# Four tiles of a convolution's output normed beside its second chunk, two of them kept in DRAM in between

## The chip, the cores and the metric

The kernel runs on one core of a Trainium2 chip. The time is that of one launch on the device, in microseconds (us), as the median of several runs. Profiles are single executions recorded by the hardware; their times count from the first instruction.

## The reference

One step of a two-layer backbone. There are 256 context tokens (the prompt, "p") and 2048 latent tokens ("s"), 1024 channels, all in float32. Layer 0 is a gated convolution branch, layer 1 is neighbourhood attention; both end in an output projection that is scaled by a gate and added to the residual. The change lies in layer 0:

```python
def conv_branch(h, w_in, dw_w, dw_b, ln_g, ln_b, w_out):
    a, b, z = jnp.split(h @ w_in, 3, axis=-1)
    u = a * jax.nn.sigmoid(b)
    u = lax.conv_general_dilated(u, dw_w[:, None, :], ...,     # 31 taps along the tokens,
        feature_group_count=CONV_WIDTH) + dw_b                 # each channel by itself
    u = layer_norm(u, ln_g, ln_b)
    u = jax.nn.silu(u) * jax.nn.silu(z)
    return u @ w_out

x = x + gate * conv_branch(rms_norm(x) * (1 + scale) + shift, ...)
```

## The kernel before

Matrix products run at full precision as three products of float32r halves (high x high, high x low, low x high), so every operand exists as a "hi" and a "lo" tile. TensorE multiplies; the others prepare operands and take results out of PSUM.

**The convolution (`conv_layer`).** The tokens are worked in two chunks: the prompt with latent tokens 0 to 1023, then latent tokens 1024 to 2047. In each chunk the 1024 channels are taken in eight steps of 128. A step projects a, b and z (the `ci_ps` products, L360 to L362) into two PSUM banks in turn, ScalarE applies the sigmoid (L474), VectorE multiplies (L476), z goes to DRAM (`zc_d`). The 31 taps are then summed: pairs as differences on VectorE into two PSUM accumulators (`cv`, L530 and L532, pool `acc`), the rest as scaled copies on ScalarE (L509) and additions on GpSimd (L512). Two joins (L536) put them together, and the result goes to DRAM (`vc_d`, L539). The steps are written as events with times on a clock of their own; sorting them gives the order of the instructions on TensorE, ScalarE, VectorE and GpSimd, which is kept (`manual_schedule`). SyncE issues the loads and stores, in an order that the scheduler chooses.

**The norm (`norm_stages`).** For a tile of 128 tokens it loads the convolution's output v and z from DRAM (L706, L708; these need the stores of all eight steps), sums over channels (L712), spreads the mean by a matmul with a matrix of ones (L720), subtracts it (L722), squares (L725), sums again (L712), gets the variance (L731), the reciprocal root (L734 to L737) and spreads it (L740), scales (L744), applies SiLU to z (L742) and to v (L747), multiplies both (L753), and rounds the product y into its hi and lo halves on GpSimd (`round_pool` L105, `rest_pool` L108). It is a generator with stages, so that a caller can lay the stages between other work.

Two prompt tiles are normed within the second chunk: `LN_FIRST`, `LN_GAP` and `LN_TIMES` place their stages on the events' clock. They use three of the four parts of a work buffer (`ln_work`), their y goes to `ln_y`. The first latent tile is normed behind `conv_layer` by `conv_norm` (L760), in the same work buffer, and its y takes two of the `t4` tiles, of which there are eight (`"t4": 8`, 4 KB per partition each). The conv weights, the gates (one for the prompt, one for the latent tokens) and wide norms use `t4` too.

**The output pipeline (`conv_out_pipeline`).** Eight tiles of 128 tokens (the prompt's two, then latent tokens 0 to 767) are projected by `w_out`, one in each pass of the loop (variable `i`). A pass holds 48 matmuls in four quarters (L848 and L849 with yh, L851 with yl), the residual additions of two halves (L857, L858), the store of x1, the root mean square of the result, and transposes (L304) for the next layer. Between the quarters stand the stages of the norms of later tiles: the loop starts tile i + 3, and tile i + 3's mean is the first of TensorE's matmuls in pass i + 1. The order on TensorE is the written one; the other engines are ordered by the scheduler. These norms take v and y from `t4`, z from `raw`, and PSUM from the pool `lnps`, which is opened when `acc` is closed. Residual tiles (`x1`) of passes 0 and 1 lie in `t4`, those of later passes in `xp`, a pool that is opened after the taps' buffers (`convp`) are closed.

Of the kernel before, what the change touches and what calls it, by code (L numbers as in the profile page):

```python
# [11 lines left out]
F32 = mybir.dt.float32  # L12
F32R = mybir.dt.float32r
# [5 lines left out]
P = 128  # L19
D = 1024  # L20
NK = D // P
# [17 lines left out]
DVE_PACE = 1.1  # L39
ADA_TIME = 3.1  # L40
ACT_FIRST = 0.5
LN_FIRST = 2
LN_GAP = 66.0
LN_TIMES = (0, 6, 14, 18, 21, 25, 33, 37, 47, 49, 52, 54, 54.1, 60, 62)
ADA_AHEAD = 4.0
ADA_LAG = 3.5
LEAD = 1.9
# [28 lines left out]
class Kern:  # L76
    def __init__(self, ctx, tc, io):
        self.tc, self.nc, self.io = tc, tc.nc, io
        self.ctx = ctx
        self.more, self.more_bufs, self.turn = None, 0, 0  # L80
        self.cp = ctx.enter_context(tc.tile_pool(name="consts", bufs=1))
        self.dr = ctx.enter_context(tc.tile_pool(name="scratch", bufs=1, space=bass.MemoryType.DRAM))
        d = lambda name, shape: self.dr.tile(shape, F32, name=name, tag=name)
        self.zc_d = d("zc_d", [D, NTOK])
        self.wl_d = d("wl_d", [3 * NK, P, D])
        self.vc_d = d("vc_d", [2, D, VCOLS // 2])
        self.x1_d = d("x1_d", [NTOK, D])
        self.qh_d = d("qh_d", [D, NTOK])
        self.ql_d = d("ql_d", [D, NTOK])
        self.ks_d = d("ks_d", [NH, 2, DH, NTOK])  # L90
        self.vp_d = d("vp_d", [NPR, NH, 2, DH])
        self.vs_d = d("vs_d", [GW // CW, NSA // GW, CW, NH, 2, DH])
        self.bm_d = d("bm_d", [NH, 3, P, 3, 480])
        self.zn_d = d("zn_d", [D, NTOK])
        self.kc_d = d("kc_d", [NH, 2, DH, NCTX])
        self.cvs_d = d("cvs_d", [NCTX, NH, 2, DH])
        self.w2_d = d("w2_d", [2, D, D])
        self.x2_d = d("x2_d", [NTOK, D])
        self.gate_d = d("gate_d", [2, 2, D])
        self.rpb_d = d("rpb_d", [P + 1, RPB_PITCH])  # L100
        self.yp_d = d("yp_d", [NK, 2, P, NPR])


    def round_pool(self, out, src):
# [260 lines left out]
    def conv_layer(self, part_a, part_b):  # L365
# [7 lines left out]
        at = lambda t, f: events.append((t, len(events), f))  # L373
# [257 lines left out]
        at(begin[NK] + 1, room)  # L631

        self.ready = []
        for j in range(2):

            st = {}

            def norm(st=st, j=j):
                if "g" not in st:
                    work, y = self.room  # L640
                    st["g"] = self.norm_stages("p", P * j, self.ready, [work[:, i] for i in range(3)] + [y[:, 2 * j + i] for i in range(2)])
                next(st["g"], None)

            for dt in LN_TIMES:
                at(begin[NK + LN_FIRST] + 2 + LN_GAP * j + dt, norm)
# [42 lines left out]
        for _, _, f in sorted(events, key=lambda e: e[:2]):  # L688
            f()

    def norm_stages(self, src, t0, y, room=None, wide=False):


        nc = self.nc
# [60 lines left out]
        yh, yl = room[3:] if room else (self.t4(F32R, nm + t) for t in ("_yh", "_yl"))  # L755
        self.round_pool(yh, z)
        self.rest_pool(yl, z, yh)
        y.append((yh, yl))

    def conv_norm(self, src, t0, room=None):  # L760
        y = []
# [63 lines left out]
    def conv_out_pipeline(self, w, blocks, ready, ahead, res):  # L825
# [39 lines left out]
        for i in range(len(tiles) + 2):  # L865
            src, a = names[i]
            run = i < len(tiles)
            if run:
                x1[i] = self.t4(F32, f"x1_{src}{a}", [P, D]) if i < 2 else self.xp.tile([P, D], F32, tag="ln", name=f"x1_{src}{a}", bufs=5)
                nc.sync.dma_start(x1[i], self.tok_rows(src, a, P))  # L870
            t, before = i + 2, i + 1
            norm(t + 1, True)
            if run:
                pm = self.mm_bank(f"co_{src}{a}_0")
            if i == 0:
                quarter(i, 0, 0, pm)
                norm(t, True)
                norm(t)
            norm(t)
            norm(before)  # L880
            if 0 < i < len(tiles):
                quarter(i, 0, 0, pm)
            norm(t)
            norm(before)
            norm(t)
            norm(before)
            scale = None
            if last:
                residual(*last)
            norm(t)  # L890
            more()
            if run:
                quarter(i, 0, 1, pm)
            norm(t)
            norm(before)
            norm(t)
            if last:
                scale = self.store_x1(i - 1, names[i - 1], x1, tiles, prep, res)
                last = None
            norm(before)  # L900
            if run:
                residual(i, 0, pm)
                more()
                pm = self.mm_bank(f"co_{src}{a}_1")
                quarter(i, 1, 0, pm)
            norm(t)
            more()
            if run:
                quarter(i, 1, 1, pm)
                last = i, 1, pm  # L910
            norm(t)
            if scale:
                scale()
            norm(t + 1)
            more()
# [427 lines left out]
    def phase1(self):  # L1343
        tc = self.tc
        with ExitStack() as c:
# [5 lines left out]
            with tc.tile_pool(name="convp", bufs=2) as self.up, tc.tile_pool(name="acc", bufs=2, space=bass.MemoryType.PSUM) as self.pc:  # L1351
# [2 lines left out]
                with tc.manual_schedule(engines=ordered):  # L1354
                    self.conv_layer([("p", 0, 256), ("s", 0, 512), ("s", 512, 512)], [("s", 1024, 512), ("s", 1536, 512)])
                work = self.room[0]
                self.ready.append(self.conv_norm("s", 0, [work[:, i] for i in range(3)] + [self.t4(F32R, f"ln_s0_y{t}") for t in "hl"]))
                self.gate = [self.spread_row(self.t4(F32, f"gate0_{g}", [P, D]), self.gate_d[0, g]) for g in range(2)]
                w = [[], []]
                for _ in self.out_weight(self.io["conv_w_out"][0], "co", w):  # L1360
# [474 lines left out]
```

## Time and profile before

| | |
|---|---|
| median of 3 runs | 2816.69 us (2813.48 to 2820.18) |
| profiled execution | 2823.78 us, span 2821.9 us, granted TensorE clock 0.984 |
| TensorE busy | 2699.2 us, 96% of the span |
| VectorE, ScalarE, GpSimd busy | 1764.9, 1377.1, 1392.8 us |
| DMA | 533.86 MB, mean 189 GB/s |

Times in the profile are microseconds from the span's start. PE is TensorE, PEld its weight loads, DVE VectorE, ACT ScalarE, POOL GpSimd, SP SyncE, and SPq its queue, which issues DMAs. L706 is line 706 of the kernel before. A row of the timeline has start, duration, engine, line, operation, output and inputs, and in brackets the idle time before it and what ended it. Tiles are named without their numbers, so that `ln_s` is any norm of latent tokens.

### The profile page before, as it was taken

The numbers are of one execution on the slowest core, as the hardware profiler recorded it, in microseconds if no ns is written. First come the engines' busy times: TensorE is split into PE (matmuls) and PEld (weight loads), VectorE is DVE, ScalarE is ACT, GpSimd is POOL, SyncE is SP. The second block draws the span as 40 slices with busy tenths as digits, with TensorE's granted clock in tenths as the row PEclk, the third lists the DMA queues.
The fourth block names the chain that finished last, engine by engine and source line by source line (L and its number), as shares of the span: only waits on it lengthen the run. The fifth ranks groups of instructions, "written<-read, shape, count | busy, mean of one in ns | idle before, by whom it ended". The sixth has DMA issues, their size and how long they took to land.

```text
span 2821.9 us, 45216 instructions
## 1 busy us (share of the span) xinstructions
PE 2699.2 (96%) x16079; PEld 2336.9 (83%) x16079; DVE 1764.9 (63%) x3046; ACT 1377.1 (49%) x2436; POOL 1392.8 (49%) x1569
## 2 busy tenths in 40 slices
PE   6999999999899999999999999989999999899998
PEld 4888877776777889999998888878888898788887
DVE  4678778888885610012456522368787787778885
ACT  3446454456453322234222244256676676667764
POOL 4687776566454343355123235134455454455564
PEclk9999999999999999999999999999999999999999
DMA  7233554555546554446789986688676768966763
GB/s 256 68 128 113 180 189 151 166 185 186 166 115 179 159 159 135 127 146 194 240 297 337 364 245 192 206 227 221 180 199 197 195 176 207 243 186 181 199 167 109
DMA packets 445337, 533.86 MB, mean 189 GB/s; under 512 B 79665, under 2 KB 322441, under 8 KB 444984
## 3 DMA queue, kind: packets, MB, share of 16 engines
q1 hardware_dynamic: 440368, 510.11, 61.3%
q10 hardware_dynamic: 4744, 20.85, 1.9%
q8 instruction: 128, 2.10, 0.3%
q14 instruction: 97, 0.79, 0.1%
HBM read 355.14 MB, written 179.79 MB: 190 GB/s over the span
## 4 chain that ended last, share of the span: by engine, by line
PE 73%; DMA 10%; DVE 5%; SPq 4%; ACT 3%; POOL 3%; issue 3%; POOLq 0%; ACTq 0%; DVEq 0%
PE sa_T L1603 7%; PE ci_ps L360 6%; PE ci_ps L361 6%; PE ci_ps L362 6%; PE sa_O L1632 5%; PE sa_O L1627 4%; PE ni_s L361 4%; PE ni_s L362 4%; PE ni_s L360 4%; PE sa_S L1571 4%; PE sa_S L1570 3%; PE o L1725 2%; PE o L1727 2%; PE o L1726 2%; DMA bm_d<-bm 2%
## 5 line engine op out<-in xcount | busy, mean ns | idle before, releaser
L1597 POOL TENSOR_SCALAR sa_p<-sa_p,sa_m 128x992 f32<-128x992 f32 (+2 forms) x256 | 276.8, 1081 | 431.5 <-DVE sa_m L1596 304.7
L512 POOL TENSOR_TENSOR cv_p<-cv_p,cv_p 128x640 f32<-128x640 f32 (+1 forms) x240 | 359.1, 1496 | 120.6 <-ACT cv_p L509 107.7
L1612 ACT CAST sa_pt<-sa_T 128x512 fp32r<-128x512 f32 (+3 forms) x512 | 275.3, 588 | 211.3 <-PE sa_T L1603 208.3
L111 DVE TENSOR_TENSOR sa_pt<-sa_T,sa_pt 128x512 fp32r<-128x512 f32 (+3 forms) x512 | 328.5, 683 | 2.4 <-ACT sa_pt L1612 2.2
L360 PE MATMUL ci_ps<-h_s_hi,ci_wh 128*128 128x512 f32 x768 | 308.9, 402 | 7.5 <-ACT z L479 3.7
L361 PE MATMUL ci_ps<-h_s_lo,ci_wh 128*128 128x512 f32 x768 | 304.2, 396 | 0.0
L362 PE MATMUL ci_ps<-h_s_hi,ci_wl 128*128 128x512 f32 x768 | 304.2, 396 | 0.0
L1595 ACT ACTIVATE sa_p<-sa_S,sa_m 128x992 f32<-128x992 f32 (+2 forms) x256 | 267.1, 1043 | 57.0 <-DVE sa_m L1591 49.4
L1603 PE MATMUL sa_T<-ident,sa_p 128*128 128x128 f32 (+3 forms) x2048 | 273.6, 276 | 9.7 <-DVE sa_pt L111 9.3
L1589 DVE TENSOR_REDUCE sa_m<-sa_S 128x1 f32<-128x512 f32 x256 | 176.2, 688 | 165.5 <-PE sa_S L1571 153.4
L1603 PEld LDWEIGHTS sa_T<-ident,sa_p 128*128 128x128 f32 (+3 forms) x2048 | 238.3, 138 | 47.1 <-issue 16.8
L509 ACT ACTIVATE cv_p<-u,ws 128x640 f32<-128x640 f32 (+1 forms) x256 | 190.8, 777 | 134.2 <-DVE u L476 98.6
L532 DVE SCALAR_TENSOR_TENSOR cv<-u,dw,cv 128x640 f32<-128x640 f32 (+1 forms) x240 | 196.2, 817 | 0.5
L1632 PE MATMUL sa_O<-sa_pt,a_v 120*128 120x256 f32 (+5 forms) x1280 | 190.7, 279 | 0.0
L360 PEld LDWEIGHTS ci_ps<-h_s_hi,ci_wh 128*128 128x128 f32 x768 | 146.2, 190 | 47.6 <-ACT z L479 6.9
L532 DVE SCALAR_TENSOR_TENSOR cv<-cv_d,dw,cv 128x640 f32<-128x640 f32 (+1 forms) x224 | 182.8, 816 | 0.0
L1627 PE MATMUL sa_O<-sa_pt,cv 128*128 128x256 f32 x1024 | 175.8, 294 | 5.3 <-ACT sa_pt L1612 1.1
L1591 DVE CUSTOM_DVE_ANT_0 sa_S<-sa_S,a_bm,sa_m 128x480 f32<-128x480 f32 (+2 forms) x256 | 170.9, 668 | 9.0
L362 PEld LDWEIGHTS ci_ps<-h_s_hi,ci_wl 128*128 128x128 f32 x768 | 145.9, 190 | 34.0
L361 PEld LDWEIGHTS ci_ps<-h_s_lo,ci_wh 128*128 128x128 f32 x768 | 146.4, 191 | 31.2
L1632 PEld LDWEIGHTS sa_O<-sa_pt,a_v 120*128 120x128 f32 (+2 forms) x1280 | 167.3, 191 | 0.0
L360 PE MATMUL ni_s<-h_s_hi,nis_wh 128*128 128x512 f32 x384 | 150.5, 392 | 2.2 <-ACT ni_s_f L1032 1.4
(798 smaller groups left out, 7143.0 us busy)
## 6 DMA issues: line engine op xcount, KB each, us to landing
adaw<-in_ada_w SPq DMA_DIRECT2D x24, 1024.0 KB
ci_w<-in_conv_w_in SPq DMA_DIRECT2D x48, 512.0 KB
a_bm<-bm_d SPq DMA_DIRECT2D x32, 720.0 KB
x_s<-in_x_sample SPq DMA_DIRECT2D x32, 512.0 KB
vs_d<-v_s SPq DMA_DIRECT2D x128, 128.0 KB
a_qh<-qh_d SPq DMA_DIRECT2D x128, 128.0 KB
a_ql<-ql_d SPq DMA_DIRECT2D x128, 128.0 KB
o_x<-x_d SPq DMA_DIRECT2D x32, 512.0 KB
```

The lines of the kernel that those rows point to most:

```text
L111: self.nc.vector.tensor_tensor(out=lo, in0=src, in1=hi.bitcast(F32), op=ALU.subtract)
L360: self.nc.tensor.matmul(out, wh[:, k, :], hh[:, k, :], start=k == 0, stop=False)
L361: self.nc.tensor.matmul(out, wh[:, k, :], hl[:, k, :], start=False, stop=False)
L362: self.nc.tensor.matmul(out, wl[:, k, :], hh[:, k, :], start=False, stop=k == NK - 1)
L512: nc.gpsimd.tensor_tensor(out=st["t", 0], in0=st["t", 0], in1=st["t", j], op=ALU.add)
L532: nc.vector.scalar_tensor_tensor(out=st["acc", b], in0=d, scalar=w, in1=st["acc", b], op0=ALU.mult, op1=ALU.add)
L1595: nc.scalar.activation(p[:, n], S[:, n], AF.Exp, scale=-1.0, bias=m[:, 2:3], accum_out=m[:, 3:4])
L1597: nc.gpsimd.tensor_scalar(out=p[:, n], in0=p[:, n], scalar1=m[:, 3:4], scalar2=1.0, op0=ALU.mult, op1=ALU.mult)
L1603: nc.tensor.transpose(t[:w, c * P : c * P + P], p[:, x + c * w : x + c * w + w], self.ident)
L1612: nc.scalar.copy(pt[:w, 0, part, :, at], t)
L1627: nc.tensor.matmul(o, cv[:, c].rearrange("p s d -> p (s d)"), x, start=s + c == 0, stop=False)
L1632: nc.tensor.matmul(dst, v[:w, c0 + c].rearrange("p s d -> p (s d)"), loc[:, lo:hi], start=False, stop=s == 1 and c == 3)
```

## The change

- The norms within the second chunk are four instead of two: the prompt's tiles and latent tokens 0 to 127 and 128 to 255. They begin one step earlier (`LN_FIRST` 1), follow each other at 48 instead of 66, and their stages are closer by the same ratio.
- The y of the two new tiles is written into the third and fourth part of the work buffer (the third also holds the squares) and stored in DRAM (`y_d`, four stores of 512 KB, `put_away`). In the pipeline, one pass ahead of its use, each is fetched into two `xp` tiles (four loads of 512 KB in all).
- The norm behind the convolution is that of latent tokens 256 to 383, the pipeline's fifth tile. The norms within the pipeline begin with its sixth tile, so that passes 0 and 1 hold no norm, and there are five instead of seven.
- Residual tiles of passes 0 to 3 lie in `t4`, not only those of 0 and 1.

```diff
@@ -39,9 +39,9 @@
 DVE_PACE = 1.1
 ADA_TIME = 3.1
 ACT_FIRST = 0.5
-LN_FIRST = 2
-LN_GAP = 66.0
-LN_TIMES = (0, 6, 14, 18, 21, 25, 33, 37, 47, 49, 52, 54, 54.1, 60, 62)
+LN_FIRST = 1
+LN_GAP = 48.0
+LN_TIMES = (0, 4.5, 10.5, 13.5, 16, 19, 25, 28, 35.5, 37, 39.5, 41, 41.1, 45.5, 47)
 ADA_AHEAD = 4.0
 ADA_LAG = 3.5
 LEAD = 1.9
@@ -99,6 +99,7 @@
         self.gate_d = d("gate_d", [2, 2, D])
         self.rpb_d = d("rpb_d", [P + 1, RPB_PITCH])
         self.yp_d = d("yp_d", [NK, 2, P, NPR])
+        self.y_d = d("y_d", [2, 2, P, D])
 
 
     def round_pool(self, out, src):
@@ -631,14 +632,15 @@
         at(begin[NK] + 1, room)
 
         self.ready = []
-        for j in range(2):
+        for j, (src, t0) in enumerate((("p", 0), ("p", P), ("s", 0), ("s", P))):
 
             st = {}
 
-            def norm(st=st, j=j):
+            def norm(st=st, j=j, src=src, t0=t0):
                 if "g" not in st:
                     work, y = self.room
-                    st["g"] = self.norm_stages("p", P * j, self.ready, [work[:, i] for i in range(3)] + [y[:, 2 * j + i] for i in range(2)])
+                    to = [y[:, 2 * j + i] for i in range(2)] if j < 2 else [work[:, i].bitcast(F32R) for i in (3, 2)]
+                    st["g"] = self.norm_stages(src, t0, self.ready, [work[:, i] for i in range(3)] + to, then=None if j < 2 else self.put_away)
                 next(st["g"], None)
 
             for dt in LN_TIMES:
@@ -688,7 +690,21 @@
         for _, _, f in sorted(events, key=lambda e: e[:2]):
             f()
 
-    def norm_stages(self, src, t0, y, room=None, wide=False):
+    def put_away(self, yh, yl):
+
+        at = self.y_d[len(self.ready) - 2]
+        for s, y in enumerate((yh, yl)):
+            self.nc.sync.dma_start(at[s], y.bitcast(F32).rearrange("p k t -> p (k t)"))
+
+        def fetch():
+            ys = [self.xp.tile([P, NK, P], F32R, tag="ln", name=f"ln_back{s}", bufs=5) for s in "hl"]
+            for s, y in enumerate(ys):
+                self.nc.sync.dma_start(y.bitcast(F32).rearrange("p k t -> p (k t)"), at[s])
+            return tuple(ys)
+
+        return fetch
+
+    def norm_stages(self, src, t0, y, room=None, wide=False, then=None):
 
 
         nc = self.nc
@@ -755,7 +771,7 @@
         yh, yl = room[3:] if room else (self.t4(F32R, nm + t) for t in ("_yh", "_yl"))
         self.round_pool(yh, z)
         self.rest_pool(yl, z, yh)
-        y.append((yh, yl))
+        y.append(then(yh, yl) if then else (yh, yl))
 
     def conv_norm(self, src, t0, room=None):
         y = []
@@ -866,10 +882,12 @@
             src, a = names[i]
             run = i < len(tiles)
             if run:
-                x1[i] = self.t4(F32, f"x1_{src}{a}", [P, D]) if i < 2 else self.xp.tile([P, D], F32, tag="ln", name=f"x1_{src}{a}", bufs=5)
+                x1[i] = self.t4(F32, f"x1_{src}{a}", [P, D]) if i < 4 else self.xp.tile([P, D], F32, tag="ln", name=f"x1_{src}{a}", bufs=5)
                 nc.sync.dma_start(x1[i], self.tok_rows(src, a, P))
             t, before = i + 2, i + 1
             norm(t + 1, True)
+            if out.get(before) and callable(out[before][0]):
+                out[before] = [out[before][0]()]
             if run:
                 pm = self.mm_bank(f"co_{src}{a}_0")
             if i == 0:
@@ -1354,7 +1372,7 @@
                 with tc.manual_schedule(engines=ordered):
                     self.conv_layer([("p", 0, 256), ("s", 0, 512), ("s", 512, 512)], [("s", 1024, 512), ("s", 1536, 512)])
                 work = self.room[0]
-                self.ready.append(self.conv_norm("s", 0, [work[:, i] for i in range(3)] + [self.t4(F32R, f"ln_s0_y{t}") for t in "hl"]))
+                self.ready.append(self.conv_norm("s", 2 * P, [work[:, i] for i in range(3)] + [self.t4(F32R, f"ln_s256_y{t}") for t in "hl"]))
                 self.gate = [self.spread_row(self.t4(F32, f"gate0_{g}", [P, D]), self.gate_d[0, g]) for g in range(2)]
                 w = [[], []]
                 for _ in self.out_weight(self.io["conv_w_out"][0], "co", w):
```

## The prediction

> **What bounds the kernel now.** I read the page first (busy shares, then the chain that ended last), then the busy time by stage around the places where the diff works, then what TensorE waited for there, and last the rows of the engines behind the longest wait.
>
> ```profile
> PE 2699.2 (96%) x16079; PEld 2336.9 (83%) x16079; DVE 1764.9 (63%) x3046; ACT 1377.1 (49%) x2436; POOL 1392.8 (49%) x1569
> ```
> ```profile
> PE 73%; DMA 10%; DVE 5%; SPq 4%; ACT 3%; POOL 3%; issue 3%; POOLq 0%; ACTq 0%; DVEq 0%
> ```
>
> TensorE is busy for 96% of the span and carries 73% of the chain. A change elsewhere is worth only what it takes from TensorE's remaining idle time, or puts there. The diff works in three stretches: the second chunk of the convolution (about 440 to 717 us), the tail of the taps (717 to 737), and the pipeline of eight output tiles (717 to 837). I call one pass of the pipeline's loop a round, and number the tiles of 128 tokens 0 to 9 in the loop's order: 0 and 1 are the prompt, 2 is latent token 0, and so on.
>
> ```profile
> core 0: us, PE busy (x) PEld busy (x) DVE busy (x) ACT busy (x) POOL busy (x), PEclk, DMA share, GB/s
> 696.00:737.00 41.00, 29.81 (x121) 23.59 (x121) 39.87 (x48) 18.29 (x24) 23.73 (x13) 0.90 0.61 190
> 717.00:737.00 20.00, 11.38 (x51) 9.00 (x49) 19.40 (x25) 4.32 (x5) 3.52 (x3) 0.87 0.55 160
> 739.00:749.00 10.00, 10.00 (x41) 8.14 (x40) 4.67 (x7) 2.10 (x3) 2.86 (x4) 0.84 0.70 264
> 763.00:789.00 26.00, 25.49 (x125) 20.64 (x124) 23.44 (x29) 16.13 (x33) 16.73 (x20) 1.00 0.54 135
> 789.00:837.00 48.00, 43.62 (x206) 35.50 (x204) 38.25 (x45) 25.26 (x51) 25.06 (x30) 0.96 0.41 114
> ```
>
> The columns are the stretch, its length and each engine's busy time, then granted clock, DMA share and GB/s. From 696 to 737 VectorE is full (39.87 of 41) while TensorE is not; from 717 TensorE has only 11.38 of 20. Later both are nearly full. What TensorE waited for between 717 and 900 (total, times, longest):
>
> ```profile
> PE ln_s_mu L720 <- DVE cv_p L536: 8.6, 1, 8.6
> PE ln_s_rb L740 <- DVE ln_s_dg L737: 3.1, 2, 2.6
> PE ln_s_var L731 <- DVE ln_s_s L712: 2.1, 4, 1.3
> ```
>
> One wait is larger than the rest together. TensorE's own rows show where it sits:
>
> ```profile
> 717.21 0.40 PE L848 MATMUL co_p<-co_h,ln_y 128*128 128x512 f32 x1
> ...
> 727.30 1.07 PE L851 MATMUL co_p<-co_h,ln_y 128*128 128x512 f32 x4
> 737.00 0.80 PE L720 MATMUL ln_s_mu<-ln_s_s,ones 128*128 128x128 f32 x2 [8.62 <-DVE cv_p L536]
> ```
> ```profile
> 751.18 0.38 PE L720 MATMUL ln_s_mu<-ln_s_s,ones 128*128 128x128 f32 x2
> ```
> ```profile
> 763.04 0.27 PE L720 MATMUL ln_s_mu<-ln_s_s,ones 128*128 128x128 f32 x1
> ```
> ```profile
> 776.07 0.27 PE L720 MATMUL ln_s_mu<-ln_s_s,ones 128*128 128x128 f32 x1
> ```
> ```profile
> 788.92 0.27 PE L720 MATMUL ln_s_mu<-ln_s_s,ones 128*128 128x128 f32 x1
> ```
> ```profile
> 800.78 0.55 PE L740 MATMUL ln_s_rb<-ln_s_dg,ones 128*128 128x128 f32 x1 [2.61 <-DVE ln_s_dg L737]
> ```
> ```profile
> 805.64 0.27 PE L720 MATMUL ln_s_mu<-ln_s_s,ones 128*128 128x128 f32 x1
> ```
>
> Round 0 lasts from 717.21 to 728.37 (11.2 us). Round 1 opens with the mean of tile 3 (L720), and waits 8.62 us for the last join of the taps (L536): the norms' PSUM banks are opened where the taps' accumulators lay. From then on rounds begin at L720: 751.18, 763.04, 776.07, 788.92, 805.64. Round 1 took 14.18 us and round 2, with as many matmuls and no wait, 11.86: the wait leaves 2.3 us of slower matmuls behind it. So 10.9 us is the most that the removal of this wait gives.
>
> **The change, part by part.**
>
> *Two more norms in the second chunk.* Tiles 2 and 3 (latent tokens 0 to 255) are normed there, tile 4 takes the place of tile 2 after the taps. What one norm costs is in the rows of the work buffer (count, then min/median/max in ns; L712 is a sum, L722 and L744 take off the mean and scale, L753 multiplies by the gate path):
>
> ```profile
> L712 DVE TENSOR_REDUCE ln_p_s<-ln_work x4: 1979/2016/2036, 496.7 to 587.0; 128x128 f32<-128x1024 f32 x4
> ...
> L753 DVE TENSOR_TENSOR ln_work<-ln_work x3: 1226/1668/1886, 553.9 to 677.1; 128x1024 f32<-128x1024 f32 x3
> L722 DVE TENSOR_TENSOR ln_work<-ln_work,ln_p_mu x2: 1211/1211/1211, 509.6 to 578.4; 128x1024 f32<-128x1024 f32 x2
> L744 DVE TENSOR_TENSOR ln_work<-ln_work,ln_p_rb x2: 1211/1211/1211, 546.4 to 615.1; 128x1024 f32<-128x1024 f32 x2
> ```
>
> VectorE: two sums at 2.0, two passes at 1.2, one at 1.7, about 8.1 us; ScalarE the squares and SiLU; GpSimd two passes for y; SyncE three loads and now two stores of 512 KB. Two norms add some 16 us of VectorE over about 200 us, and the cover there is VectorE's wait for TensorE:
>
> ```profile
> DVE u L476 <- PE ci_ps L362: 29.3, 11, 5.1
> ```
> ```profile
> PE ci_ps L360 <- ACT u L474: 1.8, 1, 1.8
> PE ci_ps L360 <- DVE shift L248: 1.1, 1, 1.1
> ```
>
> 29.3 us in 11 waits, so the arithmetic is hidden. Not hidden are the collisions of queues in written order: with two norms in this stretch TensorE lost 1.8 us behind ScalarE's sigmoid and 1.1 us behind VectorE, 2.9 us; two more could cost as much again or nothing. I take +1.5 (0 to 5, the upper end with the matmul slowdown that followed the 8.62 us wait added). If the cover is gone, VectorE's L476 is late, the two matmul banks stay full and TensorE waits for them. The stores and the fetches, 8 x 512 KB, pass on a DMA that is 0.5 to 0.7 busy; on SyncE's queue each stands behind GpSimd's rest pass, where weight loads queue behind it; the code asks for those 13 to 18 us ahead of use, so I cost that at nothing (0 to 1).
>
> *No norm in rounds 0 and 1.* The first norm in the pipeline is now tile 5, loaded in round 2, with its mean at the head of round 3. The 8.62 and 2.3 us go: -10.9, and round 1 can end at 728.4 + 11.2 = 739.6.
>
> *Tiles 2 and 3 come back from DRAM.* Round 2 needs both halves of tile 2, which are fetched into buffers that lie where the taps' were. The nearest rows are the loads into that space now:
>
> ```profile
> 736.97 0.32 SPq L539 DMA_DIRECT2D vc_d<-cv_p  x1
> 739.09 2.28 SPq L870 DMA_DIRECT2D x_s<-in_x_sample  x5
> 752.10 1.00 SPq L706 DMA_DIRECT2D ln_s_v<-vc_d  x2
> ```
> ```profile
> 763.01 0.36 SPq L706 DMA_DIRECT2D ln_s_v<-vc_d  x1
> ```
> ```profile
> 850.31 5.80 DMA x_s<-in_x_sample
> ```
>
> The last store of the taps is issued at 736.97 and the first load into their space at 739.09, 2.1 us later. Five loads of 512 KB then pass at 264 GB/s, 2.0 us each; another load of x_s is 5.8 us on the chain. So a fetch lands 2.0 to 5.8 us after 739.09; I take 4.0, between. Then the taps end later: tile 4's norm needs tile 3's work buffers, which the written schedule frees 29 us later than it frees tile 1's for tile 2 now (349.8 + 144 + 47 against 384.2 + 66 + 62 on its own clock), and brings its whole 8.1 us of VectorE into the full stretch that ends at 737, where tile 2 leaves about 3 (the L744 and L753 passes and a small one). That is +5 if all of it comes before the last tap and 0 if none: I take 2.6. Round 2 then begins at 739.1 + 2.6 + 4.0 = 745.7, a wait of 6.1, and with 2.3 us of slow matmuls behind it +8.4 (ends: +1.4 without slowdown, with the early landing and taps as now, and +13 with 5.8 and 5). Behind the waiting matmul stand all of round 2's, in TensorE's fixed order, and the residual adds on VectorE wait for them; behind the waiting fetch on SyncE's queue stand the loads of later tiles, which have a round to spare.
>
> *Four residual tiles and the fifth's y in the eight t4 buffers.* This is the place I trust least. Rows on who gets a buffer:
>
> ```profile
> 751.38 0.69 DVE L857 TENSOR_TENSOR co_op<-co_p,gate 128x512 f32<-128x512 f32 x1 [1.05 <-PE co_p L851]
> ```
> ```profile
> 778.48 1.23 DVE L753 TENSOR_TENSOR ln_s_z<-ln_s_v,ln_s_z 128x1024 f32<-128x1024 f32 x1
> ```
> ```profile
> 762.16 2.40 POOL L108 TENSOR_TENSOR ln_s_yl<-ln_s_z,ln_s_yh 128x1024 fp32r<-128x1024 f32 x1 [1.62 <-PE co_s L849]
> ```
> ```profile
> 772.64 0.38 PE L740 MATMUL ln_s_rb<-ln_s_dg,ones 128*128 128x128 f32 x2
> ```
>
> The load of tile 5 at 752.10 followed the last use of the prompt's gate (751.38), tile 3's yl (762.16) and tile 6's load (763.01) followed TensorE's last reads of tile 2: t4 is full, and buffers go out in program order. In the new round 3 it must hold one gate, y of tile 4 (2), the residual tiles 0 to 3 (4) and the inputs of tiles 5 and 6 (2): nine. The ninth gets its buffer only when tile 5's input is done. Tile 5's L740 in round 3 (763.04) is at 772.64 and its last product L753 at 778.48 to 779.7: 16.7 us after the round began, where the round itself lasts 13.0. If the ninth is tile 4's yl, it is late by 3.7 + 2.4 (L108) less the 1.8 us of matmuls that open the round, 4.3, and some of that is gained because VectorE is less loaded: I take 3.2, slow matmuls included (0 to 6). If it is tile 6's input, see the rivals.
>
> A page of the Trainium skill bears on the slow matmuls ("TensorE: Matmul & The Clock Gate", Part 1): the clock is halved only after an idle window of about 3.4 us. By it waits of 2 to 3 us would cost their length alone and this term 2.2 instead of 3.2. The trace speaks against a firm bound: the round with the 2.61 us wait (800.78) lasted 16.72 against 12.85 for the one before, 1.3 us more than the wait.
>
> *Later rounds.* Rounds 5 to 7 fill the stretch from 789 to 837, 48 us where three rounds of 13 are 39: TensorE's small waits (L740 3.1, L731 2.1) and slow matmuls behind them make most of the 9. With two norms less in the queue of GpSimd and VectorE part of it may go; the same buffers may bring a new wait in round 5, when tile 7's input needs the buffer of residual 0. I take -2 (-9 to +3).
>
> **Sum.** -10.9 + 8.4 + 3.2 + 1.5 - 2.0 = +0.2 us against the profiled execution's own 2823.78 (span 2821.9). That execution stands 7.1 us above the median shown, 2816.69; what changes is a local difference, so I carry it over: about 2817. After the pipeline nothing is touched, and a shift of TensorE passes to the end, since it is near full throughout. A difference of 0.2% (5.6 us) is about what a measurement of this kernel can tell from no change; the three runs shown spread by 6.7.
>
> **Rivals.**
>
> *Faster: the buffers do not bite.* If the residual of tile 3 gives way, or GpSimd and VectorE finish tile 5 within the round, the 3.2 is gone; if also the taps end at 737 as now, the fetch costs 3.5 and 2.3 of slow matmuls, and the later rounds give 4: -10.9 + 5.8 + 1.5 - 4 = -7.6, 2809; with every bound the good way -14, 2803. For it: from 763 to 789 VectorE has 23.44 of 26 with a norm in every round, so with none it has room in rounds 0 to 2. Against: tile 5's chain hangs on matmuls at fixed places of TensorE's order, which less load does not move.
>
> *Slower: tile 6's input is the ninth.* The residual tile 3 stands before it in the program, so it would take the gate's buffer, and tile 6 would wait for tile 5's product, 3.7 us past the end of round 3. Then two loads (2 to 4 us) and a sum (2.0 us) stand before the mean at the head of round 4, which TensorE cannot pass: 3.7 + 3 + 2 = 8.7, less some 1.4 for a lighter VectorE, with 2.3 behind it +9.6 in place of 3.2. The sum is +6.6, 2823; with late taps and collisions in the chunk +13, 2830. It decides as soon as this wait passes 9 us. For it: the order of the rows above. Against: tile 4's y may be ready so late that it is the ninth.
>
> *The change does nothing there.* If the fetch waits for another part of the old space, or late taps hold round 2 until about 751, the wait has only moved from round 1 to round 2: -10.9 + 13 + 1.5 = +3.6, 2820, still no change.
>
> **How the numbers follow.** No change 0.38 (the forecast, with the moved wait in it), faster 0.31, slower 0.31: the two rivals hang on the same buffers, and the rows do not say which user comes ninth. Those two ends give 2803 and 2830; I leave out a tenth at each side: 2804 to 2829. The forecast alone would range from 2812 to 2822.
>
> **What would show it.** Right: no L720 wait in round 1; round 1 begins at once after round 0; L848 at the head of round 2 waits 3 to 9 us for the fetched tile, whose loads are issued some 2 us after the last store of the taps; the last L536 comes 0 to 5 us later against the end of the convolution's matmuls; a wait at the head of round 4, for yl (then L851) or for the mean (then L720). In the chunk VectorE's waits at L476 shrink from 29.3 by about 16, TensorE's grow by less than 5. The prediction is wrong if round 2 begins with no wait, or if in round 4 there is none, or if VectorE in the chunk comes to hold TensorE's banks.

## The result, and the profile after

The changed kernel takes 2849.01 us (median; 2847.83 to 2855.09) beside 2815.09 for the kernel before in the same comparison: a ratio of 1.0136, 95% interval 1.0113 to 1.0158. It is slower by 34 us between these medians (the recorded ratio, which is not their quotient of 1.0120, would make it 38); the forecast was 2817, with a range of 2804 to 2829. The profiled execution of the changed kernel spans 2846.0 us. All line numbers below are those of the changed kernel, which lie higher than those of before: the norm's sum L712 is now L728, its mean matmul L720 is L736, the output products L848 to L851 are L864 to L867, the weights' rest co_l is L112.

The busy shares and the chain of the changed kernel:

```profile
PE 2692.8 (95%) x16079; PEld 2329.0 (82%) x16079; DVE 1763.4 (62%) x3046; ACT 1380.8 (49%) x2438; POOL 1392.5 (49%) x1569
...
PE 35%; DMA 2%; DVE 2%; ACT 1%; issue 1%; SPq 1%; POOL 0%; POOLq 0%; DVEq 0%; ACTq 0%
```

TensorE does the same 16079 matmuls, but the chain, which TensorE carried to 73% before, is followed here through only some two fifths of the span (the shares of its line add up to 42%). So the page alone does not locate the loss; the stages do. First the rows of TensorE that open the second chunk, the pipeline, and the first products after it, in the kernel before and in the changed one:

```profile
447.13 1.06 PE L225 MATMUL ada_ps<-adaw,cs 128*32 128x512 f32 x8
```
```profile
860.36 0.50 PE L360 MATMUL ni_s<-h_s_hi,nip_wh 128*128 128x512 f32 x1
```
```profile
438.44 1.49 PE L226 MATMUL ada_ps<-adaw,cs 128*32 128x512 f32 x12
```
```profile
715.60 0.40 PE L864 MATMUL co_p<-co_h,ln_y 128*128 128x512 f32 x1
```
```profile
882.57 0.39 PE L361 MATMUL ni_s<-h_s_hi,nip_wh 128*128 128x512 f32 x1
```

With 717.21 as the first output product of before, the second chunk lasts 270.1 us before and 277.2 after (+7.1), the pipeline 143.1 and 167.0 (+23.8), and what follows to the end of the span 1961.5 and 1963.4 (+1.9). The stretch ahead of the chunk is 8.7 us shorter in the changed kernel's execution; none of the changed lines works there (the last section returns to it). Without that stretch the stages give +32.8, and the medians +33.9.

What TensorE waited for from 712 to 900 us in the changed kernel (total, times, longest), and two of the stretches shown of before:

```profile
PE ln_s_mu L736 <- DVE ln_s_s L728: 14.7, 2, 10.5
PE co_p L865 <- DVE co_l L112: 11.0, 6, 6.1
PE co_p L864 <- ACT co_h L790: 5.4, 2, 3.7
```
```profile
717.00:737.00 20.00, 6.28 (x12) 3.17 (x12) 19.11 (x23) 5.91 (x7) 8.06 (x5) 0.68 0.62 196
...
763.00:789.00 26.00, 21.45 (x102) 17.47 (x101) 12.54 (x19) 8.31 (x18) 7.83 (x12) 1.00 0.47 150
```

The 8.62 us behind the last join of the taps are gone, and two others stand in their place: 16.4 us (11.0 + 5.4) for the output weights, and 14.7 us for the sum of a norm. From 717 to 737 TensorE does 12 matmuls where it did 51, at a granted clock of 0.68 (0.87 before); from 763 to 789 VectorE is busy for 12.5 of 26 us where it was for 23.4, and no engine is full. The rows of the first rounds:

```profile
716.54 0.39 PE L864 MATMUL co_p<-co_h,ln_y 128*128 128x512 f32 x1
717.96 0.49 PE L865 MATMUL co_p<-co_l,ln_y 128*128 128x512 f32 x1 [1.03 <-DVE co_l L112]
722.16 0.80 PE L864 MATMUL co_p<-co_h,ln_y 128*128 128x512 f32 x1 [3.71 <-ACT co_h L790]
724.28 0.79 PE L865 MATMUL co_p<-co_l,ln_y 128*128 128x512 f32 x1 [1.32 <-DVE co_l L112]
...
728.74 0.50 PE L865 MATMUL co_p<-co_l,ln_y 128*128 128x512 f32 x1 [1.54 <-DVE co_l L112]
...
735.67 0.80 PE L865 MATMUL co_p<-co_l,ln_y 128*128 128x512 f32 x1 [6.08 <-DVE co_l L112]
...
741.21 0.79 PE L865 MATMUL co_p<-co_l,ln_y 128*128 128x512 f32 x1 [0.47 <-DVE co_l L112]
...
744.73 0.39 PE L865 MATMUL co_p<-co_l,ln_y 128*128 128x512 f32 x1
...
749.55 0.39 PE L864 MATMUL co_p<-co_h,ln_y 128*128 128x512 f32 x1
```

Round 0 takes 715.60 to 749.55, 33.95 us, where it took 11.16. In it stand the 16.4 us of waits; the other 6.4 are slow matmuls (0.80 us at 735.67 against 0.39 at 716.54). Round 1 then runs from 749.55 to 760.54 without a wait: 11.0 us in place of 22.8. Then the second new wait, in the order in which it arises (SyncE's queue, VectorE, TensorE):

```profile
784.26 1.00 SPq L722 DMA_DIRECT2D ln_s_v<-vc_d  x2
```
```profile
793.03 1.87 DVE L728 TENSOR_REDUCE ln_s_s<-ln_s_v 128x128 f32<-128x1024 f32 x1 [5.32 <-DMA ln_s_v<-vc_d]
```
```profile
794.96 0.80 PE L736 MATMUL ln_s_mu<-ln_s_s,ones 128*128 128x128 f32 x2 [10.51 <-DVE ln_s_s L728]
```
```profile
813.76 0.76 PE L736 MATMUL ln_s_mu<-ln_s_s,ones 128*128 128x128 f32 x2 [4.18 <-DVE ln_s_s L728]
```

The load of tile 6's values is issued at 784.26, VectorE sums them at 793.03, 8.8 us later, and the mean that opens round 4 waits 10.51 us; the one that opens round 5 waits 4.18. Rounds 3 and 4 together take 42.0 us (771.75 to 813.76) where they took 25.9 (763.04 to 788.92). So the pipeline's +23.8 is +22.8 (round 0), -11.8 (round 1), -0.7 (round 2), +16.1 (rounds 3 and 4) and -2.6 (after them).

Why are the weights late? First the row of the first co_l in the kernel before; then, in the changed kernel, the load that opens the norm behind the taps, that norm's product on VectorE and its last pass on GpSimd, and the first and the last co_l:

```profile
689.86 2.31 DVE L111 TENSOR_TENSOR co_l<-co_raw,co_h 128x1024 fp32r<-128x1024 f32 x1 [0.36 <-POOL ln_s_yl L108]
```
```profile
661.66 0.37 SPq L722 DMA_DIRECT2D ln_work<-vc_d  x1
```
```profile
706.12 1.21 DVE L769 TENSOR_TENSOR ln_work<-ln_work 128x1024 f32<-128x1024 f32 x1
```
```profile
714.40 2.42 POOL L109 TENSOR_TENSOR ln_s_yl<-ln_work,ln_s_yh 128x1024 fp32r<-128x1024 f32 x1
```
```profile
707.25 1.21 DVE L112 TENSOR_TENSOR co_l<-co_raw,co_h 128x1024 fp32r<-128x1024 f32 x1
```
```profile
739.93 1.23 DVE L112 TENSOR_TENSOR co_l<-co_raw,co_h 128x1024 fp32r<-128x1024 f32 x1 [1.04 <-ACT co_h L790]
```

Before, co_l starts at 689.86, 0.36 us of waiting behind the last pass (yl) of tile 2's norm. Now the norm behind the taps (tile 4) begins with its load at 661.66, because it stands behind tile 3's in the same work buffer, and ends at 716.8; co_l starts at 707.25, 17.4 us later, and the eighth at 739.93 (717.37 before): 24.3 us after the first output product, where it started 0.2 us after it. The norm's values lie in the work buffer, which is one of the four "slot" buffers; the output weights need all four. Yet the first co_l does not wait for that buffer here: it follows the norm's product (L769) on VectorE without a pause, and two pieces of it are written by 709.6, while GpSimd reads that product out of the work buffer until 716.8. What sets its time in this trace is its place in VectorE's order, which the scheduler chose, and the trace does not tell why. The fifth experiment gives the norm other buffers.

### The profile page after: what moved, and what is told of

Its sections match the earlier page's. It is cut to its first block, busy times and chain, and to the rows that moved or that the text cites. A ratio compares the mean times of both kernels' runs of the same rounds, so it can differ in the third digit from the quotient of the medians.

```text
span 2846.0 us, 45222 instructions
## 1 busy us (share of the span) xinstructions
PE 2692.8 (95%) x16079; PEld 2329.0 (82%) x16079; DVE 1763.4 (62%) x3046; ACT 1380.8 (49%) x2438; POOL 1392.5 (49%) x1569
## 5 line engine op out<-in xcount | busy, mean ns | idle before, releaser
L1615 POOL TENSOR_SCALAR sa_p<-sa_p,sa_m 128x992 f32<-128x992 f32 (+2 forms) x256 | 277.7, 1085 | 431.1 <-DVE sa_m L1614 300.2
L112 DVE TENSOR_TENSOR sa_pt<-sa_T,sa_pt 128x512 fp32r<-128x512 f32 (+3 forms) x512 | 328.5, 683 | 2.5 <-ACT sa_pt L1630 2.2
L361 PEld LDWEIGHTS ci_ps<-h_s_hi,ci_wh 128*128 128x128 f32 x768 | 145.4, 189 | 52.9 <-ACT u L475 10.4
L363 PEld LDWEIGHTS ci_ps<-h_s_hi,ci_wl 128*128 128x128 f32 x768 | 145.4, 189 | 33.7
```

What stands on the lines that cost most here:

```text
L112: self.nc.vector.tensor_tensor(out=lo, in0=src, in1=hi.bitcast(F32), op=ALU.subtract)
L361: self.nc.tensor.matmul(out, wh[:, k, :], hh[:, k, :], start=k == 0, stop=False)
L363: self.nc.tensor.matmul(out, wl[:, k, :], hh[:, k, :], start=False, stop=k == NK - 1)
L1615: nc.gpsimd.tensor_scalar(out=p[:, n], in0=p[:, n], scalar1=m[:, 3:4], scalar2=1.0, op0=ALU.mult, op1=ALU.mult)
```

## The experiments

**The residual tiles as before.** The change, but only the two prompt tiles' residuals in t4.

```diff
-x1[i] = self.t4(...) if i < 4 else self.xp.tile(...)
+x1[i] = self.t4(...) if i < 2 else self.xp.tile(...)
```

> The changed kernel, but residual tiles 2 and 3 lie in xp again, so that t4 must hold at most eight. Buffers theory (the ninth t4 tile delays tile 6's input, 10.5 us of wait at the head of round 4 and 4.2 in round 5): both waits go, with the slow matmuls behind them some 16 us, so the time is 2831 to 2835, still 16 to 20 above the kernel before, and the waits for the output weights in round 0 (16.4 us) stay. Weights theory alone (all of the loss is the late low halves of the output weights in round 0, and the later waits are only its echo): within 5 us of the changed kernel, 2844 to 2854. A third way: the fifth xp buffer is short now, and residual 3 waits for tile 2's halves, which shows as a new wait in round 3 or 4 and takes back a part.

Measured: 2838.48 us, ratio 1.0101 (1.0077 to 1.0124), 0.35% less than the change, some 10 us. TensorE's waits from 712 to 900:

```profile
PE co_p L865 <- DVE co_l L112: 10.5, 6, 5.6
PE co_p L864 <- ACT co_h L790: 7.3, 3, 3.7
```

The time is 3.5 us above the range of the buffers theory, and the waits are as it said. The wait for the mean is gone, in round 4 and in round 5, and nothing of its size has taken its place; the pipeline is 153.6 us long, 13.4 less. The wait for the weights stays, 17.8 us in sum. So the t4 buffers cost 10 to 13 us, by the mechanism of the slower rival, and they are not the whole.

**No norm behind the taps.** The change without tile 4's norm there (four tiles are normed before the pipeline, tile 4 is its first).

```diff
-self.ready.append(self.conv_norm("s", 2 * P, [work[:, i] for i in range(3)] + ...))
```

> The changed kernel without the norm behind the taps: tile 4 is normed in the pipeline, beginning in round 1. Weights theory (the norm behind the taps holds the work buffer from 626 to 717 us instead of to 690, so that the low halves of the output weights find no place and VectorE makes them 17 us late; 16.4 us of waits in round 0): round 0 takes 11 to 13 us again, round 2 waits 3 to 5 us for the fetched tile, and the wait at the head of round 4 stays; some 15 us less than the changed kernel, 2832 to 2838. Buffers theory alone: round 0 may be whole, but the wait at the head of round 4 grows by as much, 2846 to 2852.

Measured: 2829.24 us, ratio 1.0065 (1.0046 to 1.0083), 0.71% less than the change, some 20 us, and 3 us below the lower end of the weights theory's range. Round 0 now runs through; rounds 2, 4 and 5 wait:

```profile
748.19 0.74 PE L864 MATMUL co_s<-co_h,ln_backh 128*128 128x512 f32 x1 [2.74 <-issue]
```
```profile
780.84 2.08 PE L867 MATMUL co_s<-co_h,ln_s_yl 128*128 128x512 f32 x4 [3.92 <-POOL ln_s_yl L109]
```
```profile
797.85 0.77 PE L736 MATMUL ln_s_mu<-ln_s_s,ones 128*128 128x128 f32 x2 [4.19 <-DVE ln_s_s L728]
```

The fetch of tile 2 (ln_backh, the operand of the waiting matmul; the trace puts the wait down to "issue") holds TensorE for 2.74 us. It is issued at 744.59, 2.1 us behind the last store of the taps at 742.51. This is the wait that the prediction had put into the change, and that the late round 0 hides there. The t4 buffers cost two waits here. Round 4 waits 3.92 us for the low half of tile 4's y: its high half is made at 765.43, and GpSimd begins the low one at 778.45, just behind tile 5's product on VectorE (777.00 to 778.22). Round 5 waits 4.19 us for a mean. The third experiment, with fewer tiles in t4, has neither. So here the ninth tile is the one that the prediction had in its sum.

**Both edits.**

> Both edits at once: no norm behind the taps, residual tiles 2 and 3 in xp. If the two theories are separate and together the whole loss in the pipeline (23.8 us longer there than before): the pipeline is some 6 us shorter than before, the second chunk 5 to 7 us longer, and the time is 2808 to 2820, no change against the kernel before. If a third cost lies in the fetches or in the order of VectorE: above 2825.

Measured: 2815.83 us, ratio 1.0021 (1.0006 to 1.0035). The two causes add up: 0.35% and 0.71% are 1.06%, and both together take 1.15%. The pipeline lasts 134.8 us, 8.3 less than before, with the fetch's wait of 2.5 us in it: this is what the removal of the 8.62 us wait gives. But the second chunk lasts 280.7 us against 270.1, and that eats it. Where, is seen in the waits of TensorE in the chunk and at the longest of them, on ScalarE and TensorE:

```profile
PE ci_ps L361 <- ACT u L475: 8.3, 4, 4.0
PE ci_ps L361 <- DVE adao L238: 3.4, 1, 3.4
PE ci_ps L361 <- DVE shift L249: 2.5, 1, 2.5
```
```profile
601.50 3.18 ACT L763 ACTIVATE ln_work<-ln_work,more 128x128 f32<-128x128 f32 x8
...
605.32 1.28 ACT L475 ACT_TABLE_LOAD   x1
606.61 0.60 ACT L475 ACTIVATE u<-ci_ps 128x512 f32<-128x512 f32 x1
```
```profile
607.26 0.79 PE L361 MATMUL ci_ps<-h_s_hi,ci_wh 128*128 128x512 f32 x1 [4.05 <-ACT u L475]
```

14.2 us in these three, where the kernel before loses 6.9 in all its waits there. (The second, 3.4 us, is not among the changed kernel's waits; it is there once the norm behind the taps is left out, and with it the chunk is 3.5 us longer than the change's.) ScalarE finishes a norm's SiLU (L763, 3.18 us for eight) at 604.7, loads another table (1.28) and comes to the sigmoid at 606.61; the matmul bank that waits for it holds TensorE for 4.05 us.

**Two norms, at the new times.** The kernel before with only the three constants of the schedule changed.

```diff
-LN_FIRST = 2
-LN_GAP = 66.0
+LN_FIRST = 1
+LN_GAP = 48.0
```

(and the list of fifteen times, as in the change).

> The kernel before with only the three constants changed (the prompt's two norms begin one step earlier and are closer together); no norm is added, none moved. Chunk theory A (the second chunk is 6.7 us longer because its queues collide where the norms now begin and how dense they are): 2 to 5 us slower than before, with the waits behind ScalarE's sigmoid grown. Chunk theory B (it is the number of norms): no change within 3 us. Should the norm behind the taps begin earlier for it, some gain of the order of 2 us could show in round 1.

Measured: 2807.83 us, ratio 0.9993 (0.9977 to 1.001): no change. The chunk is 271.2 us long, and the wait for the last join stays:

```profile
PE ln_s_mu L720 <- DVE cv_p L536: 8.1, 1, 8.1
```

TensorE's wait behind the sigmoid grew in the chunk (6.5 us, 1.8 before), but others shrank. So the closer times cost the chunk about 1 us by themselves; the rest of its 7 to 10 us comes with the third and fourth norm.

**A place of its own for tile 4's norm.** The first experiment's kernel, with the norm's three working tiles in t4.

```diff
-self.conv_norm("s", 2 * P, [work[:, i] for i in range(3)] + ...)
+self.conv_norm("s", 2 * P, [self.t4(F32, f"ln_s256_{t}") for t in "vzq"] + ...)
```

> Edit: the first experiment's kernel (residual tiles 2 and 3 outside t4, 1.0101 of before), but tile 4's norm behind the taps keeps its values in three t4 buffers of its own instead of the work buffer of the second chunk. The arithmetic of that norm on VectorE, ScalarE and GpSimd stays, and so does its place in the program. Buffer theory: the output weights (co_h, co_l) come late because the norm holds the work buffer, which is one of their four places, until its yl is done at 716.8. With a place of its own the work buffer is free when tile 3's y is stored, co_l comes before 707, the co_l and co_h waits of round 0 (10.5 + 7.3 us in the first experiment's kernel) fall below 3 together, and the time falls by 14 to 20 us, to 2818 to 2824. Rival, VectorE's load: the weights are late because tile 4's 8 us of VectorE fill the stretch to 717 together with the taps; the arithmetic is all there still, so the waits stay over 10 us and the time stays within 4 us of 2838.

Measured: 2819.48 us, ratio 1.0027 (1.0012 to 1.0042), 0.74% less than the first experiment's: as much as leaving the norm out gave, with all its arithmetic still there. VectorE's first co_l, and TensorE's rows:

```profile
694.53 2.09 DVE L112 TENSOR_TENSOR co_l<-co_raw,co_h 128x1024 fp32r<-128x1024 f32 x1
```
```profile
723.51 0.51 PE L865 MATMUL co_p<-co_l,ln_y 128*128 128x512 f32 x1 [0.47 <-DVE co_l L112]
...
738.45 0.77 PE L864 MATMUL co_p<-co_h,ln_y 128*128 128x512 f32 x1 [7.99 <-DVE co_op L873]
```
```profile
741.55 0.75 DVE L537 SCALAR_TENSOR_TENSOR cv_p<-cv,more,cv_p 128x520 f32<-128x520 f32 x1
```

co_l starts at 694.53 while the norm is still at its first sum, and TensorE waits 0.47 us for weights. So it is not the amount of the norm's work on VectorE that cost round 0 its 17 us. It fits that it was the buffer that the norm holds, but the edit moved more than that: the norm's load is issued at 684.39 (661.66 in the change) and its product comes at 731.81 (706.12), behind all eight co_l. Buffer and order changed together, and no run tells them apart. What the time on VectorE costs is here too: the last join of the taps is at 741.55 (736.18 before), the scaling of round 0's products (L873) stands among the taps, and round 1 waits for it 7.99 us. It is the old wait of 8.62 us under another name: with a norm's arithmetic behind the taps, VectorE is behind, and round 1 meets it through whichever buffer it needs. The third experiment, without that norm, has no wait in round 1.

**SiLU between the sigmoids.** The kernel with both edits, the four norms' times in the chunk laid one by one.

```diff
-LN_TIMES = (0, 4.5, ..., 47)
+LN_HEAD = (0, 4.5, 10.5, 13.5, 16, 19, 25, 28, 35.5)
+LN_PLAN = ((0, (43, ...)), (50, (38.5, ...)), (100, (45.5, ...)), (152, (36.5, ...)))
```

> Edit: the third experiment's kernel (no norm behind the taps, residual tiles 2 and 3 outside t4, 1.0021 of before), with the times of the four norms in the second chunk laid so that each norm's two SiLU stages on ScalarE fall between two sigmoids (starts 0, 50, 100, 152 instead of every 48, and late stages at 36 to 52). The same work. Collision theory: TensorE's waits for ScalarE's sigmoid (1.5 + 1.4 + 4.1 us in the third experiment's kernel) come from a SiLU and its table load just ahead of the sigmoid; they fall below 2 us in sum, the second chunk becomes 4 to 7 us shorter, and the time is 2807 to 2812. Rival, the amount: four norms are too much for VectorE and GpSimd in this stretch whatever their place; the waits only move, and the time stays within 2 us of 2816.

Measured: 2816.97 us, ratio 1.0017 (1.0002 to 1.0032): the time of the rival. Yet the chunk did become shorter, 272.8 us against 280.7, more than the 4 to 7 expected; the waits for the sigmoid fell from 8.3 to 5.8 only, those for the adaLN row from 3.4 to 1.1. The pipeline gave it back: 145.4 us against 134.8, behind the weights once more:

```profile
PE co_p L866 <- DVE co_l L113: 10.7, 3, 3.9
```

The convolution's matmuls end 8 us earlier against the start of the chunk, while the eighth co_l starts 7 us later in it. Tile 3's y leaves the work buffer 7 us later too, but it does so in the seventh experiment as well (both begin its store at 678.8), where TensorE waits 3.0 us for the weights; so that alone does not explain it. Neither theory is right as stated: the collisions were real, but behind them stand the weights, which bound the start of the pipeline here, and what holds them stays open.

**Both, with tile 4's norm in a place of its own.**

> Edit: the sixth experiment's kernel with tile 4's norm put back behind the taps, its values in three t4 buffers of its own: the change as it was meant, with both buffer conflicts taken out and the norms' SiLU laid between the sigmoids. If the two buffers and the collisions are all that the change cost, the time lies within 3 us of the sixth experiment's, or up to 6 below it, since one norm less stands in the pipeline; no wait over 4 us is left between 717 and 860. If VectorE's load behind the taps costs by itself, the last join of the taps comes later by 3 to 8 us against the end of the convolution's matmuls, and the time is 5 to 10 us above the sixth's.

Measured: 2815.75 us, ratio 1.0005 (0.9987 to 1.0023): level with before. Chunk 275.5, pipeline 138.6. Four waits are left in rounds 0 and 1, 6.1 us in sum; the longest is the one on VectorE's scaling, as in the fifth:

```profile
PE co_p L865 <- DVE co_op L874: 3.0, 1, 3.0
```

**One norm less in the chunk.** The seventh's kernel with tiles 0 to 2 in the chunk and tile 3 behind the taps.

```diff
-for j, (src, t0) in enumerate((("p", 0), ("p", P), ("s", 0), ("s", P))):
+for j, (src, t0) in enumerate((("p", 0), ("p", P), ("s", 0))):
...
-self.conv_norm("s", 2 * P, ...)
+self.conv_norm("s", P, ...)
```

> Edit: the seventh experiment's kernel with one norm less in the second chunk: tiles 0, 1 and 2 there (tile 2's y in DRAM), tile 3 behind the taps with three t4 buffers of its own, tile 4 first in the pipeline with its mean at the head of round 2. The seventh lies at 1.0005 of before. Here the work buffer is free some 50 us earlier and VectorE has 8 us less before the taps end. If what is left of the cost is the number of norms in the chunk (its chunk was 275.5 us against 270.1 of before), the chunk falls to 271 to 273 and the time to 2806 to 2811, 0.1 to 0.3% under before. If the number does not matter any more, and the end of the taps on VectorE bounds round 1 (a wait of 3 us there in the seventh's trace), the time stays within 2 us of before, 2811 to 2815. Slower than before by over 5 us if the mean of tile 4 waits at the head of round 2 for its load.

Measured: 2821.63 us, ratio 1.0027 (1.0012 to 1.0041): 0.22% above the seventh, though the two intervals overlap, and the expected gain did not come. By the medians it is 9 us slower than before, as the last of the three cases had it, but not for its reason: no mean waits at the head of round 2. The chunk is no shorter (277.7 us): tile 3's norm begins 12 us earlier in it than the seventh's norm behind the taps (mean at 685.4, the chunk's start at 441.3; 702.8 and 446.8 there), and TensorE waits at that norm's own matmuls, 3.80 us at the longer. And with rounds 0 and 1 on time the fetch of tile 2 comes to light:

```profile
705.99 0.49 PE L757 MATMUL ln_s_rb<-ln_s_dg,ones 128*128 128x128 f32 x2 [3.80 <-DVE ln_s_dg L754]
```
```profile
747.78 0.77 PE L865 MATMUL co_s<-co_h,ln_backh 128*128 128x512 f32 x1 [6.25 <-DMA ln_backh<-y_d]
```

None of the eight beats the kernel before. The table holds them side by side; the kernel before had a median of 2811.07 us in the comparisons of 1 to 4, 2812.78 in 5 to 7 and 2812.74 in 8; chunk and pipeline are cut as above, in the one profiled execution of each.

| kernel | ratio to before | 95% interval | chunk, us | pipeline, us |
|---|---|---|---|---|
| before | 1 | | 270.1 | 143.1 |
| the change | 1.0136 | 1.0113 to 1.0158 | 277.2 | 167.0 |
| 1: residuals as before | 1.0101 | 1.0077 to 1.0124 | 277.1 | 153.6 |
| 2: no norm behind the taps | 1.0065 | 1.0046 to 1.0083 | 280.7 | 144.1 |
| 3: both | 1.0021 | 1.0006 to 1.0035 | 280.7 | 134.8 |
| 4: two norms, new times | 0.9993 | 0.9977 to 1.0010 | 271.2 | 141.1 |
| 5: first, norm in its own place | 1.0027 | 1.0012 to 1.0042 | 278.0 | 139.4 |
| 6: third, SiLU laid between | 1.0017 | 1.0002 to 1.0032 | 272.8 | 145.4 |
| 7: sixth, norm in its own place | 1.0005 | 0.9987 to 1.0023 | 275.5 | 138.6 |
| 8: seventh, three early | 1.0027 | 1.0012 to 1.0041 | 277.7 | 138.4 |

## Why the prediction was wrong

It forecast no change and gave slower 0.31; the time lies 20 us above the upper end of the range. Step by step:

*The wait that goes, -10.9.* Right. No mean waits in round 1, which falls from 22.8 to 11.0 us; the third experiment's pipeline, 8.3 us shorter with a fetch wait of 2.5 in it, gives the same sum. What was not right is "round 1 can end at 739.6": the wait was on VectorE's end of the taps, and the fifth experiment shows it again (7.99 us) as soon as the weights are on time and a norm is still behind the taps.

*The norm behind the taps, +2.6.* This step failed, and it is the largest part of the miss. It saw that tile 4's norm "needs tile 3's work buffers", and priced what that does to VectorE: the last join comes 22.5 us after the first output product (738.12 in the changed kernel) where it came 19.0 after it, so +3.5 for an estimate of 2.6. It did not ask what comes late behind that norm. The output weights do, and round 0 paid 22.8 us. (Weight loads were thought of only on SyncE's queue, behind the stores, "at nothing"; there the first load of output weights was in time, 684.16 against 682.76.) Rows that could have told it stood in the trace of before: co_l at 689.86 with "0.36 <-POOL ln_s_yl" as its releaser, and the first output product 27 us later. With the norm's end 27 us later too (716.8 against 689.8) and the first co_l 17 us later, that slack was spent. The experiments without that norm (the second) and with its values elsewhere (the fifth) show that this norm in the work buffer is the cause; whether through the buffer or through VectorE's order stays open. No rival had this, and none of the bounds reached it.

*The fetch, +8.4.* Nothing of it shows in the changed kernel, because round 0 is late: the fetch is issued from 743.78 on and round 2 begins at 760.54. Where round 0 is whole the wait is there, 2.5 and 2.74 us without a norm behind the taps, 6.25 in the eighth experiment (the forecast wait was 6.1). The mechanism was right; in the change it is covered by a larger loss.

*The ninth t4 buffer, +3.2.* The mechanism was right and, for the change, the user wrong: tile 6's input came ninth, as in the slower rival. Where no norm stands behind the taps (the second experiment), it is tile 4's yl after all, with 3.92 us of wait where the sum had 4.3. The rival's price of 9.6 compares with 10.51 and 4.18 us of waits and some 10 us of time between the change and the first experiment. That it came so near is in part luck: the load followed TensorE's last transposes of a prompt tile's residual (L305, at 784.07), at the end of round 3 and not 3.7 us past it behind tile 5's product (785.77), and from its issue to the sum passed 8.8 us where the rival had counted 2 to 4.

*The second chunk, +1.5 (0 to 5).* Too small: +7.1 in the change and up to 10.6 in the third experiment. The cover that was named, VectorE's 29.3 us of waits, was real (20.0 are left in the changed kernel, where 13 were expected), but it did not help where the queues cross, and TensorE's waits there rose from 6.9 to 11.6 us: a SiLU and its table load ahead of a sigmoid, adaLN rows and shifts on VectorE. The sixth experiment takes 7.9 us from the chunk by placing alone, of which the three waits above carry 5.3; the rest is not accounted for, and its chunk is still 2.7 us longer than before's.

*Later rounds, -2.* Right: -2.6 from round 5 to the end of the pipeline.

The terms as measured, -11.8 - 0.7 + 22.8 + 16.1 - 2.6 + 7.1 + 1.9, make +32.8. The slower rival would not have been enough without the weights either: the second experiment, where they are on time and the t4 waits are still there, is 18 us slower than the kernel before in its own comparison, and the rival had 6.6 to 13. Its time of 2829.24 lies within the rival's 2823 to 2830 only because the kernel before was faster in that comparison (2811.07 against 2816.69); its chunk alone is 10.7 us longer.

## What to carry to other kernels

When work is moved to a later time, list for every buffer that it holds who takes the buffer next, and by when, and what stands behind it in the order of each engine; a step that is free on its engine can still make late what nobody had in mind. A releaser named in the trace with a short idle time in front of it (0.36 us here) is a chain at its limit: what it releases has no slack of its own, only that of its user. And a wait for an engine that is behind is removed by taking work from that engine, not by changing the buffer through which the wait is met.

## What the runs showed of the hardware

Short waits cost more than their length once a long one has slowed the clock. In the rows of round 0 above, a wait of 1.03 us is followed by a matmul of 0.49 us, the one of 3.71 by 0.80, and the one of 1.32 by 0.79; the granted clock is 0.50 from 723 to 727 us. At 728.74 the matmul behind 1.54 us takes 0.50 again, with a granted clock of 0.93 from 727 to 731. Then comes the wait of 6.08; behind it a matmul takes 0.80, one behind 0.47 us still takes 0.79, and 0.39 comes back at 744.73, 3.5 us after the last wait. Round 0 lost 6.4 us to this beside its 16.4 us of waits. The Trainium skill, "TensorE: Matmul & The Clock Gate", Part 1, states that the clock is halved after an idle window of about 3.4 us and is given back after about as long a busy one. For the return this trace agrees, with 3.5 us of work. For the loss the 3.71 us fit, but shorter waits slow the matmuls too, so the figure is no lower bound here. The fetch's wait in the third experiment shows it:

```profile
746.20 0.53 PE L864 MATMUL co_s<-co_h,ln_backh 128*128 128x512 f32 x1 [2.50 <-issue]
746.52 0.63 PE L865 MATMUL co_s<-co_l,ln_backh 128*128 128x512 f32 x1
```

The products ahead of that wait take 0.40 us each, and those behind it 0.63 for some 3 us; behind the 2.74 us of the second experiment it is the same.

The start of the program varies without a cause in the edits. The first 440 us hold nothing of any edit, yet the first ada_ps of the second chunk comes at 438 to 442 us in the changed kernel and in experiments 1, 2, 3, 5 and 8, and at 447 in the kernel before and in experiments 4, 6 and 7. The difference lies in the first 100 us, where the granted clock differs:

```profile
60.00:80.00 20.00, 14.64 (x61) 12.04 (x62) 11.42 (x18) 6.19 (x12) 9.60 (x17) 0.74 0.17 53
```
```profile
60.00:80.00 20.00, 17.05 (x93) 14.17 (x94) 11.19 (x23) 8.35 (x17) 9.18 (x20) 0.91 0.19 59
```

The clock from 60 to 80 us is 0.74 to 0.76 in the four that start late, and 0.83 to 0.91 in the six others, with one profiled execution of each kernel. What decides between the two was not tried. The profiled execution of before, a late one, lies 9 us above the median of its comparison with the change, which fits, and it is why stages and not spans are compared here.
